# Moving columns of 512-wide products read from two halves in turn, PSUM read with a step of 2

## Chip, cores and metric

The kernel runs on one core of one Trainium2 chip. The metric is the device time of one execution in microseconds; lower is better. The time before is the median of three runs.

## What is computed

A trunk of two layers over 512 tokens with 1024 features, batch 1. Layer A mixes with a recurrent state per head (12 heads of 64) in parallel with a cross-attention into 256 memory tokens (4 heads); layer B mixes with attention in chunks of 64 tokens over the own chunk and 8 earlier ones, again beside a memory attention. Each layer then adds a gated channel mixer with a convolution over three tokens. Cut to what matters here:

```python
p = rms_norm(x, ln1[layer]) @ w_in                    # mixer columns | memory-query columns
mix = rwkv7_time_mix(h, p[..., :768 * 3], ...)        # layer A
mix = chunk_attention(q, k_pad, v_pad, bias)          # layer B
mo = memory_attention(q_mem, mem_n, w_mem_kv[layer])
x = x + concatenate([mix, mo]) @ w_out[layer]
gate, val = split(rms_norm(x, ln2[layer]) @ ffn_in[layer])
x = x + (gelu(conv3(gate)) * val) @ ffn_out[layer]
...
return rms_norm(x, ln_f)
```

All arithmetic is fp32. Large products are made of three single-pass products: each fp32 operand is split into a high part that the single pass takes exactly and a low rest, and high by high, high by low and low by high are summed in PSUM.

## The kernel before

Activations lie with features on the 128 partitions and the 512 tokens along the free axis: a tile `[128, 8, 512]` holds 1024 features. A weight tile holds 128 output features by 1024 inputs, in a high part `whi` (cast on ACT) and a low part `wlo` (subtracted on DVE, or fetched again by a DMA that adds).

`dense` makes one tile of 128 output features: for each of 8 feature blocks the weights are the stationary operand and 512 token columns are the moving one, first high weights by high and low activations (lines 241 and 242), then low weights by high activations (line 245): 24 products into one PSUM bank. It serves the projections of both mixers, the LoRA pairs, the output projections and the last tile of each channel mixer. Two banks (`psd`) take turns, so that a reader empties one while the other fills. Readers are DVE instructions for the most part: `proj` multiplies by the norm factor `rho` (line 1160), `out_proj` adds to the residual (line 407), `q_split` and `k_proj` scale queries and keys (1727 and 1742), `lora_pair`, `prepare` and `head_wide` do the like.

Stages, in order: mixer A (0 to 354 us; six head pairs, whose preparation, front and back are woven by a planner with costs written by hand), its output projection, the 21 tiles of the channel mixer's input products by a seven-product scheme with 256 columns each (`Seven`, line 434; with a last, plain tile in `ending`), and `out_by_seven`, the output products. In these, the activations are the stationary operand, 128 tokens at a time, and the weights `hi` and `lo` are the moving one, 512 output features wide (lines 698 and 703 in `rows`). Layer B repeats this with attention in place of the recurrence: `rows` in `attention` makes scores for 128 queries by 128 to 512 keys (lines 1788 and 1789), a DVE instruction adds the bias and finds the row's extreme in the same pass (line 1793), ACT exponentiates, DVE normalises, TensorE transposes, and the values are multiplied (line 1817). `mem_attention` does the same for the memory tokens; its value products (line 370) are plain fp32, not split, with 512 token columns.

The order of work on TensorE is that of the program text, with the planner's weaving of generators in the mixers. Loads of weights are issued by SyncE's queue; those that add are issued by GpSimd's.

Of the kernel before, what the change touches and what calls it, by code (L numbers as in the profile page):

```python
# [18 lines left out]
P = 128  # L19
S = 512  # L20
# [39 lines left out]
def _constants():  # L60
    f = np.float32
    c = np.zeros((P, NCST), f)

    def put(name, a):
        o, n = COFF[name]
        c[:, o:o + n] = a

    i = np.arange(P)
    same = (i[:, None] // 64) == (i[None, :] // 64)
    put("ident", np.eye(P, dtype=f))  # L70
    put("ones_d", np.full((P, 2), 1.0 / 1024, f))
# [12 lines left out]
    return c  # L84


# [35 lines left out]
def trunk_kernel(ctx, tc, A, out):  # L122
# [96 lines left out]

    def mm3(ps, wh, wl, ah, al, start, stop):  # L220
        PE.matmul(ps, wh, ah, start=start, stop=False)
        PE.matmul(ps, wh, al, start=False, stop=False)
        PE.matmul(ps, wl, ah, start=False, stop=stop)
# [6 lines left out]
    def behind_dense():  # L230
        return tc.issue_after(dense_at[0].ins)

    def dense(ps, units, act, order=None, start=True, stop=True):

        ks = [(w, j, k) for w, kk in units for j, k in enumerate(kk)]
        if order is not None:
            ks = [next(q for q in ks if q[2] == k) for k in order]

        for n, ((wh, wl), j, k) in enumerate(ks):
            ah, al = act(k)  # L240
            PE.matmul(ps, wh[:, j * P:(j + 1) * P], ah, start=start and n == 0, stop=False)  # L241
# [89 lines left out]
    def mem_attention(l, score, cost, dst, pr_tile, pt_tile):  # L331
# [66 lines left out]
    def out_proj(l, act, taken, xT, order, pre=(), done=()):  # L398
        for m in range(KD):
# [17 lines left out]
    def ffn(l, hp, U, T, new_x, xT, after=None, tokens=None):  # L417
# [29 lines left out]
        class Seven:  # L447
# [86 lines left out]
            def end5(self):  # L534
                keep(V.tensor_tensor(hid32[self.j], self.v[:], self.c[:], op=ALU.mult))

# [78 lines left out]
        def ending():  # L615
# [29 lines left out]
            g, c = tmp(), tmp()  # L645
            keep(V.tensor_tensor(g[:], pg[:], rho[:], op=ALU.mult))
            run(dense(pv[:], [(wv[:2], KO)], pair_of(Uh, Ul)))
            tile21 = Seven(j)
            tile21.g, tile21.c, tile21.v = g, c, pv
            tile21.end2()  # L650
# [41 lines left out]
        def rows(pss, act, k0, ch, first, last):  # L692
            hi, lo, n = ch
            for t, ps in pss:
                ts = slice(t * P, t * P + P)
                for i in range(n):
                    for a in act:
                        PE.matmul(ps[:], a[:, k0 + i, ts], hi[:, i * S:i * S + S],  # L698
                                  start=bool(first) and (first is True or t in first) and a is act[0] and i == 0, stop=False)
            for t, ps in pss:  # L700
                ts = slice(t * P, t * P + P)
                for i in range(n):
                    PE.matmul(ps[:], act[0][:, k0 + i, ts], lo[:, i * S:i * S + S], start=False, stop=bool(last) and t in last and i == n - 1)  # L703

# [310 lines left out]
    def lora_pair(idx, w, wm):  # L1015
# [5 lines left out]
        b_ = tmp()  # L1021
        V.tensor_tensor(b_[:], pb[:], rho[:], op=ALU.mult)
        z = tmp()
        V.tensor_tensor(z[:], pa[:], rho[:], op=ALU.mult)
        V.tensor_tensor(z[:], z[:], b_[:], op=ALU.subtract)
# [73 lines left out]
    def head_wide(src, fix, bank, tied=False):  # L1099
# [9 lines left out]
        fix(a[:], ps[:])  # L1109
        V.tensor_scalar(y[:].bitcast(I32), a[:].bitcast(I32), -0.5, 1597463007.0, op0=ALU.mult, op1=ALU.add)  # L1110
# [15 lines left out]
    def prepare(i, T):  # L1126
# [12 lines left out]
        pa = ps_s()  # L1139
        PE.matmul(pz[:], wah[:, 0], zw[:], start=True, stop=False)  # L1140
        PE.matmul(pa[:], wah[:, 1], zs[:], start=True, stop=False)
        PE.matmul(pz[:], wal[:, 0], zw[:], start=False, stop=True)
        PE.matmul(pa[:], wal[:, 1], zs[:], start=False, stop=True)
# [6 lines left out]
        SC.activation(th[:], pa[:], AF.Tanh, scale=0.5, bias=aw0h[:, i:i + 1])  # L1150

        def proj(j, nm, nxt):
# [107 lines left out]
        def bonus():  # L1260
# [7 lines left out]
            pb = ps_s()  # L1268
            PE.matmul(pb[:], blk1[:], rkh[:], start=True, stop=False)
            PE.matmul(pb[:], blk1[:], rkl[:], start=False, stop=True)  # L1270
            T["pb"] = pb
# [232 lines left out]
    def dst_mix(i, yc, pg):  # L1504
        V.tensor_tensor(yc[:], yc[:], pg[:], op=ALU.mult)
        if i < 4:
# [4 lines left out]
    def q_mem(src, act, qm):  # L1511
        for f in range(2):
            w = load_w(src(f))
            ps = ps_d()
            yield from dense(ps[:], [(w, K8)], act)
            V.scalar_tensor_tensor(qm[f], ps[:], 0.125, rho[:], op0=ALU.mult, op1=ALU.mult)

    def dst_mem(f, pso):
        SC.copy(r1h[:, 6 + f], pso[:])
        V.tensor_tensor(r1l[:, 6 + f], pso[:], r1h[:, 6 + f], op=ALU.subtract)  # L1520

# [164 lines left out]
    with ExitStack() as bctx:  # L1686
# [9 lines left out]

        def put_aside(m, src):
            t_ = tmp()
            SC.copy(t_[:], src)
            nc.sync.dma_start(mixb[m], t_[:])  # L1700
# [24 lines left out]
        def q_split(ps, T):  # L1725
            q = tmp()
            V.scalar_tensor_tensor(q[:], ps[:], 0.125, rho[:], op0=ALU.mult, op1=ALU.mult)

# [6 lines left out]
        def k_proj(i, T, ps=None):  # L1735
# [5 lines left out]
            k_ = tmp()  # L1741
            V.tensor_tensor(k_[:], ps[:], rho[:], op=ALU.mult)
            ks = ap_.tile([P, 2, S], F32R, name="ks", tag="ks")
# [29 lines left out]
        def attention(i, T):  # L1773
# [98 lines left out]
        def dst_memb(f, pso):  # L1872
            put_aside(6 + f, pso[:])
            done.add(f"m{f}")
# [85 lines left out]


def layout(i):
    g = {k: np.asarray(v) for k, v in i.items()}
# [34 lines left out]
    for l in range(2):  # L1998
# [33 lines left out]
```

## Time and profile before

| | |
|---|---|
| timed runs | 1291.62, 1292.89, 1293.07 us |
| median | 1292.89 us |
| span of the profiled execution, first to last instruction | 1292.6 us |
| granted TensorE clock, mean over the span | 0.997 |
| DMA, mean | 149 GB/s (192.14 MB) |
| HBM read | 174.20 MB |

The span leaves out what lies before the first and after the last instruction of the program; the profiled execution's span and the median of the timed runs differ by 0.3 us. In the rows of a profile "psf<-whi,th" names the tile written, then the tiles read; "128x512" is partitions by elements. A start time is counted from the start of the span. PE is TensorE, PEld its weight load, DVE VectorE, ACT ScalarE, POOL GpSimd, SP SyncE.

### The profile page before, as it was taken

Reading aid. Unit: us, or ns where it says so; the run is one execution under the profiler, and the core shown is the slowest. Engines: PE = TensorE matmul, PEld = TensorE weight load, DVE = VectorE, ACT = ScalarE, POOL = GpSimd, SP = SyncE. Lnnn points to the kernel's source line nnn. Section 1 sums busy time; section 2 is a strip of 40 time slices with the busy share of each in tenths; the row PEclk is TensorE's granted clock in tenths of the full one; section 3 lists DMA queues with packets and bytes.
Section 4 is the critical chain, followed back from the end, with each engine's and each line's share of the span. In section 5 each row is a group of like instructions: output and inputs, shape, how many; then the busy total and the mean of one; then the engine's idle time right before and its main releaser. Section 6 shows DMA issues by size and latency. Waiting matters only on the chain.

```text
span 1292.6 us, 26432 instructions
## 1 busy us (share of the span) xinstructions
PE 1260.9 (98%) x10420; PEld 1083.1 (84%) x10420; DVE 1031.7 (80%) x1956; ACT 846.4 (65%) x1398; POOL 152.7 (12%) x182
## 2 busy tenths in 40 slices
PE   9999999999999999999999999999999999999997
PEld 7887777777789999998888878787789999998886
DVE  7867677765688999998876876658889999998684
ACT  6566767856476777776554676757757777765662
POOL 1000000000001222320220000000002222211200
PEclk9999999999999999999999999999999999999999
DMA  5364444453055988996984322234429989978951
GB/s 204 110 174 106 100 96 89 92 109 96 30 166 126 212 198 198 206 208 172 274 185 122 118 87 82 76 104 123 130 61 212 197 193 211 208 161 262 233 149 66
DMA packets 95581, 192.14 MB, mean 149 GB/s; under 512 B 22112, under 2 KB 30432, under 8 KB 95456
## 3 DMA queue, kind: packets, MB, share of 16 engines
q1 hardware_dynamic: 68592, 129.14, 31.9%
q0 software_dynamic: 26864, 61.31, 27.3%
q8 instruction: 82, 1.34, 0.4%
q14 instruction: 43, 0.35, 0.1%
HBM read 174.20 MB, written 6.29 MB: 140 GB/s over the span
## 4 chain that ended last, share of the span: by engine, by line
PE 62%; DVE 15%; ACT 8%; DMA 8%; issue 6%; SPq 0%; POOL 0%; ACTq 0%; DVEq 0%; POOLq 0%
PE psf L434 8%; PE psf L698 7%; PE psd L245 6%; PE psd L241 5%; PE psd L242 5%; DMA wlv<-in_ffn_in_dram 4%; PE psf L436 4%; PE psf L703 4%; PE psd L698 3%; ACT whi L499 2%; DMA wraw<-in_ffn_in_dram 2%; PE psd L703 2%; DVE raw L486 1%; PE pss L1817 1%; DVE wlo L504 1%
## 5 line engine op out<-in xcount | busy, mean ns | idle before, releaser
L499 ACT CAST whi<-raw 128x1024 fp32r<-128x1024 f32 (+1 forms) x168 | 153.3, 942 | 62.3 <-PE psf L434 29.5
L434 PE MATMUL psf<-th,whi 128*128 128x256 f32 x672 | 161.4, 278 | 2.5 <-ACT tmp L553 1.9
L434 PE MATMUL psf<-tl,whi 128*128 128x256 f32 x672 | 161.1, 276 | 0.0
L195 ACT CAST whi<-wraw 128x1024 fp32r<-128x1024 f32 x84 | 87.6, 1048 | 78.3 <-PE psd L242 37.4
L434 PEld LDWEIGHTS psf<-th,whi 128*128 128x128 f32 x672 | 125.8, 188 | 3.9 <-ACT tmp L553 2.9
L434 PEld LDWEIGHTS psf<-tl,whi 128*128 128x128 f32 x672 | 126.0, 188 | 0.0
L504 DVE TENSOR_TENSOR wlo<-raw,whi 128x1024 fp32r<-128x1024 f32 (+1 forms) x108 | 109.3, 1012 | 9.1 <-ACT whi L499 8.9
L241 PE MATMUL psd<-r1h,whi 128*128 128x512 f32 x264 | 107.4, 408 | 0.0
L242 PE MATMUL psd<-r1l,whi 128*128 128x512 f32 x264 | 105.0, 398 | 0.0
L203 DVE TENSOR_TENSOR wlo<-wraw,whi 128x1024 fp32r<-128x1024 f32 x65 | 79.2, 1219 | 22.3 <-ACT whi L195 20.4
L688 ACT CAST whi<-raw 128x1024 fp32r<-128x1024 f32 (+1 forms) x52 | 49.6, 954 | 59.9 <-PE psf L698 33.1
L689 DVE TENSOR_TENSOR wlo<-raw,whi 128x1024 fp32r<-128x1024 f32 (+1 forms) x52 | 56.5, 1097 | 38.9 <-ACT whi L688 31.5
L436 PE MATMUL psf<-th,wlo 128*128 128x256 f32 x504 | 78.0, 276 | 0.0
L245 PE MATMUL psd<-r1h,wlo 128*128 128x512 f32 x264 | 74.3, 403 | 0.6 <-DMA wlo<-in_ffn_in_dram 0.4
L471 POOL DMA_DIRECT2D wlv<-in_ffn_in_dram x40 | 60.7, 1516 | 59.5 <-DVE tmp L572 59.1
L436 PEld LDWEIGHTS psf<-th,wlo 128*128 128x128 f32 x504 | 66.8, 188 | 0.0
L434 PE MATMUL psf<-r2h,whi 128*128 128x256 f32 x252 | 60.9, 278 | 0.7 <-ACT whi L499 0.7
L434 PE MATMUL psf<-r1h,whi 128*128 128x256 f32 x252 | 60.7, 277 | 0.7 <-ACT whi L499 0.7
L434 PE MATMUL psf<-r2l,whi 128*128 128x256 f32 x252 | 60.7, 277 | 0.0
L434 PE MATMUL psf<-r1l,whi 128*128 128x256 f32 x252 | 60.6, 277 | 0.0
L241 PEld LDWEIGHTS psd<-r1h,whi 128*128 128x128 f32 x264 | 49.6, 188 | 12.0 <-issue 2.1
L525 ACT ACTIVATE tmp<-tmp,vec 128x512 f32<-128x512 f32 x44 | 36.0, 817 | 33.3 <-DVE tmp L512 33.3
(611 smaller groups left out, 3576.8 us busy)
## 6 DMA issues: line engine op xcount, KB each, us to landing
raw<-in_ffn_in_dram SPq DMA_DIRECT2D x42, 512.0 KB, 5.2
raw<-in_ffn_in_dram SPq DMA_DIRECT2D x84, 256.0 KB, 5.5
wlv<-in_ffn_in_dram POOLq DMA_DIRECT2D x40, 512.0 KB, 8.6
raw<-in_ffn_out_dram SPq DMA_DIRECT2D x30, 512.0 KB, 6.2
raw<-in_ffn_out_dram POOLq DMA_DIRECT2D x24, 512.0 KB, 8.4
wraw<-in_wA_dram SPq DMA_DIRECT2D x20, 512.0 KB, 4.1
wraw<-in_w_out_dram SPq DMA_DIRECT2D x16, 512.0 KB, 4.1
wraw<-in_ffn_outp_dram SPq DMA_DIRECT2D x16, 512.0 KB, 4.5
```

Of the source, the lines that this page charges most:

```text
L195: high = lambda: pin(SC.copy(hi[:, :n], raw))
L203: pin(V.tensor_tensor(lo[:, :n], raw, hi[:, :n], op=ALU.subtract))
L241: PE.matmul(ps, wh[:, j * P:(j + 1) * P], ah, start=start and n == 0, stop=False)
L242: dense_at[0] = PE.matmul(ps, wh[:, j * P:(j + 1) * P], al, start=False, stop=False)
L245: dense_at[0] = PE.matmul(ps, wl[:, j * P:(j + 1) * P], act(k)[0], start=False, stop=stop and n == len(ks) - 1)
L434: PE.matmul(ps, wh[:, o + k * P:o + k * P + P], x[k][n], start=k == n == 0, stop=False)
L436: PE.matmul(ps, wl[:, ol + k * P:ol + k * P + P], x[k][0], start=False, stop=k == 3)
L471: GP.dma_start(self.low[:].rearrange("p (a s) -> p a s", a=2), self.second, accum_op=ALU.add)
L499: keep(SC.copy(hi[:, :n], self.pair(what) if n > S else self.raw[:, what]))
L504: keep(V.tensor_tensor(lo[:, :n], self.pair(what) if n > S else self.raw[:, what], hi[:, :n], op=ALU.subtract))
L698: PE.matmul(ps[:], a[:, k0 + i, ts], hi[:, i * S:i * S + S], start=bool(first) and (first is True or t in first) and a is act[0] and i == ...
L703: PE.matmul(ps[:], act[0][:, k0 + i, ts], lo[:, i * S:i * S + S], start=False, stop=bool(last) and t in last and i == n - 1)
```

## The change

Three views are added. `woven` reads a tile of n columns as column 0, column n/2, column 1, column n/2 + 1 and so on. A product whose moving operand is woven puts its results in that order, so `plain_order` reads PSUM as even columns and then odd ones, a step of 2 with two runs, and `halved` gives the other operand and the output the same shape, two contiguous halves.

The moving operand becomes woven in `dense` (where it has 512 columns), `mm3`, the value products of `mem_attention`, `rows` of the output products, `head_wide`, the four products at the head of `prepare`, the bonus, and the scores of the two wider query tiles (384 and 512 keys). For the output products no reader changes: the weights `ffn_out7` and `ffn_outp` are laid out beforehand so that the woven read gives plain order. Every other reader of such a bank takes `plain_order`. Products of 256 columns, the transposes and the values of the chunked attention stay as they are.

```diff
+def woven(t):
+    return t.rearrange("p (a b) -> p b a", a=2)
+
+def halved(t):
+    return t.rearrange("p (a b) -> p a b", a=2)
+
+def plain_order(ps):
+    return ps.rearrange("p (b a) -> p a b", a=2)
...
     def mm3(ps, wh, wl, ah, al, start, stop):
+        ah, al = woven(ah), woven(al)
...
+    def moving(hl):
+        return [woven(t) if t.shape[-1] == S else t for t in hl]
...
-            ah, al = act(k)
+            ah, al = moving(act(k))
...
-            dense_at[0] = PE.matmul(ps, wl[:, j * P:(j + 1) * P], act(k)[0], start=False,
+            dense_at[0] = PE.matmul(ps, wl[:, j * P:(j + 1) * P], moving(act(k))[0], start=False,
...
-                    PE.matmul(pso[hs, :], vm[l][:, kt, (f * 2 + hh) * 64:(f * 2 + hh + 1) * 64], pts[f, hh, kt],
+                    PE.matmul(pso[hs, :], vm[l][:, kt, (f * 2 + hh) * 64:(f * 2 + hh + 1) * 64], woven(pts[f, hh, kt]),
...
-            V.tensor_tensor(xT[:, m], xT[:, m], ps[:], op=ALU.add)
+            V.tensor_tensor(halved(xT[:, m]), halved(xT[:, m]), plain_order(ps[:]), op=ALU.add)
...
-                        PE.matmul(ps[:], a[:, k0 + i, ts], hi[:, i * S:i * S + S],
+                        PE.matmul(ps[:], a[:, k0 + i, ts], woven(hi[:, i * S:i * S + S]),
...
-                    PE.matmul(ps[:], act[0][:, k0 + i, ts], lo[:, i * S:i * S + S], start=False, stop=bool(last) and t in last and i == n - 1)
+                    PE.matmul(ps[:], act[0][:, k0 + i, ts], woven(lo[:, i * S:i * S + S]), start=False, stop=bool(last) and t in last and i == n - 1)
...
-            PE.matmul(ps[:], blk1[:], hi[:], start=True, stop=False)
-            PE.matmul(ps[:], blk1[:], lo[:], start=False, stop=True)
+            PE.matmul(ps[:], blk1[:], woven(hi[:]), start=True, stop=False)
+            PE.matmul(ps[:], blk1[:], woven(lo[:]), start=False, stop=True)
...
-        SC.activation(sig[:], pz[:], AF.Tanh, scale=0.5, bias=aw0h[:, 6 + i:7 + i])
+        SC.activation(halved(sig[:]), plain_order(pz[:]), AF.Tanh, scale=0.5, bias=aw0h[:, 6 + i:7 + i])
...
-            V.tensor_tensor(p_[:], ps[:], rho[:], op=ALU.mult)
+            V.tensor_tensor(halved(p_[:]), plain_order(ps[:]), halved(rho[:]), op=ALU.mult)
...
-        V.tensor_tensor(bon[:], T["pb"][:], T["v"][:], op=ALU.mult)
+        V.tensor_tensor(halved(bon[:]), plain_order(T["pb"][:]), halved(T["v"][:]), op=ALU.mult)
...
+                mix, flat_, sorted_ = (woven, halved, plain_order) if qt > 1 else (lambda t: t,) * 3
...
-                PE.matmul(ps[:, :n], qs[:, hh, qc], ks[:, hh, :n], start=True, stop=False)
-                PE.matmul(ps[:, :n], qs[:, hh, qc], kl[:, hh, :n], start=False, stop=True)
+                PE.matmul(ps[:, :n], qs[:, hh, qc], mix(ks[:, hh, :n]), start=True, stop=False)
+                PE.matmul(ps[:, :n], qs[:, hh, qc], mix(kl[:, hh, :n]), start=False, stop=True)
...
-                V.tensor_tensor_reduce(sb[:, :n], ps[:, :n], big[hh][:, S - n:S], -1.0, 3e38,
+                V.tensor_tensor_reduce(flat_(sb[:, :n]), sorted_(ps[:, :n]), flat_(big[hh][:, S - n:S]), -1.0, 3e38,
...
+def _woven(w):
+
+    return np.ascontiguousarray(w.reshape(*w.shape[:-1], -1, S // 2, 2).swapaxes(-1, -2)).reshape(w.shape)
...
-    A["ffn_out7"] = np.stack(seven)
-    A["ffn_outp"] = np.stack(plain)
+    A["ffn_out7"] = _woven(np.stack(seven))
+    A["ffn_outp"] = _woven(np.stack(plain))
```

The lines left out give the remaining readers of a woven bank (the last tile of the channel mixer, the LoRA pair, the memory query, the output of the memory attention, queries and keys of layer B, the gate of mixer A) the same three views, and nothing else.

More of the change, by code (lines that the diff above doesn't have):

```diff
@@ L534, in end5 @@
             def end5(self):
-                keep(V.tensor_tensor(hid32[self.j], self.v[:], self.c[:], op=ALU.mult))
+                v = self.v if self.j == NFF - 1 else halved(self.v[:])
+                keep(V.tensor_tensor(halved(hid32[self.j]), v, halved(self.c[:]), op=ALU.mult))
             def frame(self, prev2, prev, nxt, norm=None, ending=None):
@@ L645, in ending @@
             g, c = tmp(), tmp()
-            keep(V.tensor_tensor(g[:], pg[:], rho[:], op=ALU.mult))
+            keep(V.tensor_tensor(halved(g[:]), plain_order(pg[:]), halved(rho[:]), op=ALU.mult))
             run(dense(pv[:], [(wv[:2], KO)], pair_of(Uh, Ul)))
             tile21 = Seven(j)
-            tile21.g, tile21.c, tile21.v = g, c, pv
+            tile21.g, tile21.c, tile21.v = g, c, plain_order(pv[:])
             tile21.end2()
@@ L1021, in lora_pair @@
         b_ = tmp()
-        V.tensor_tensor(b_[:], pb[:], rho[:], op=ALU.mult)
+        V.tensor_tensor(halved(b_[:]), plain_order(pb[:]), halved(rho[:]), op=ALU.mult)
         z = tmp()
-        V.tensor_tensor(z[:], pa[:], rho[:], op=ALU.mult)
+        V.tensor_tensor(halved(z[:]), plain_order(pa[:]), halved(rho[:]), op=ALU.mult)
         V.tensor_tensor(z[:], z[:], b_[:], op=ALU.subtract)
@@ L1105, in head_wide @@
         with behind_dense() if tied else ExitStack():
-            PE.matmul(ps[:], blk1[:], hi[:], start=True, stop=False)
-            PE.matmul(ps[:], blk1[:], lo[:], start=False, stop=True)
+            PE.matmul(ps[:], blk1[:], woven(hi[:]), start=True, stop=False)
+            PE.matmul(ps[:], blk1[:], woven(lo[:]), start=False, stop=True)
         a, y, sh = tmp(), tmp(), tmp()
-        fix(a[:], ps[:])
+        fix(halved(a[:]), plain_order(ps[:]))
         V.tensor_scalar(y[:].bitcast(I32), a[:].bitcast(I32), -0.5, 1597463007.0, op0=ALU.mult, op1=ALU.add)
@@ L1139, in prepare @@
         pa = ps_s()
[L1140 to L1143, printed above, removed]
+        PE.matmul(pz[:], wah[:, 0], woven(zw[:]), start=True, stop=False)
+        PE.matmul(pa[:], wah[:, 1], woven(zs[:]), start=True, stop=False)
+        PE.matmul(pz[:], wal[:, 0], woven(zw[:]), start=False, stop=True)
+        PE.matmul(pa[:], wal[:, 1], woven(zs[:]), start=False, stop=True)
         yield 860
         sig = tmp()
-        SC.activation(sig[:], pz[:], AF.Tanh, scale=0.5, bias=aw0h[:, 6 + i:7 + i])
+        SC.activation(halved(sig[:]), plain_order(pz[:]), AF.Tanh, scale=0.5, bias=aw0h[:, 6 + i:7 + i])
         V.tensor_scalar(sig[:], sig[:], 0.5, 0.5, op0=ALU.mult, op1=ALU.add)
         th = kt_("a")
-        SC.activation(th[:], pa[:], AF.Tanh, scale=0.5, bias=aw0h[:, i:i + 1])
+        SC.activation(halved(th[:]), plain_order(pa[:]), AF.Tanh, scale=0.5, bias=aw0h[:, i:i + 1])
         def proj(j, nm, nxt):
@@ L1268, in bonus @@
             pb = ps_s()
-            PE.matmul(pb[:], blk1[:], rkh[:], start=True, stop=False)
-            PE.matmul(pb[:], blk1[:], rkl[:], start=False, stop=True)
+            PE.matmul(pb[:], blk1[:], woven(rkh[:]), start=True, stop=False)
+            PE.matmul(pb[:], blk1[:], woven(rkl[:]), start=False, stop=True)
             T["pb"] = pb
@@ L1504, in dst_mix @@
     def dst_mix(i, yc, pg):
-        V.tensor_tensor(yc[:], yc[:], pg[:], op=ALU.mult)
+        V.tensor_tensor(halved(yc[:]), halved(yc[:]), plain_order(pg[:]), op=ALU.mult)
         if i < 4:
@@ L1515, in q_mem @@
             yield from dense(ps[:], [(w, K8)], act)
-            V.scalar_tensor_tensor(qm[f], ps[:], 0.125, rho[:], op0=ALU.mult, op1=ALU.mult)
+            V.scalar_tensor_tensor(halved(qm[f]), plain_order(ps[:]), 0.125, halved(rho[:]), op0=ALU.mult, op1=ALU.mult)
     def dst_mem(f, pso):
-        SC.copy(r1h[:, 6 + f], pso[:])
-        V.tensor_tensor(r1l[:, 6 + f], pso[:], r1h[:, 6 + f], op=ALU.subtract)
+        SC.copy(halved(r1h[:, 6 + f]), plain_order(pso[:]))
+        V.tensor_tensor(halved(r1l[:, 6 + f]), plain_order(pso[:]), halved(r1h[:, 6 + f]), op=ALU.subtract)
     def flush_mix():
@@ L1695, in trunk_kernel, with put_aside @@
         nc.sync.dma_start(vm1, kv1[1])
-        def put_aside(m, src):
+        def put_aside(m, src, view=lambda t: t):
             t_ = tmp()
-            SC.copy(t_[:], src)
+            SC.copy(view(t_[:]), src)
             nc.sync.dma_start(mixb[m], t_[:])
@@ L1726, in q_split @@
             q = tmp()
-            V.scalar_tensor_tensor(q[:], ps[:], 0.125, rho[:], op0=ALU.mult, op1=ALU.mult)
+            V.scalar_tensor_tensor(halved(q[:]), plain_order(ps[:]), 0.125, halved(rho[:]), op0=ALU.mult, op1=ALU.mult)
             qs = ap_.tile([P, 2, S], F32R, name="qs", tag="qs", bufs=3)
@@ L1741, in k_proj @@
             k_ = tmp()
-            V.tensor_tensor(k_[:], ps[:], rho[:], op=ALU.mult)
+            V.tensor_tensor(halved(k_[:]), plain_order(ps[:]), halved(rho[:]), op=ALU.mult)
             ks = ap_.tile([P, 2, S], F32R, name="ks", tag="ks")
@@ L1872, in dst_memb @@
         def dst_memb(f, pso):
-            put_aside(6 + f, pso[:])
+            put_aside(6 + f, plain_order(pso[:]), halved)
             done.add(f"m{f}")
```

## The prediction

> **What bounds the kernel now.** I read the page first (busy times, then the chain that ended last), then the busy time by stretches, cut where the stages change.
>
> ```profile
> PE 1260.9 (98%) x10420; PEld 1083.1 (84%) x10420; DVE 1031.7 (80%) x1956; ACT 846.4 (65%) x1398; POOL 152.7 (12%) x182
> ...
> PE 62%; DVE 15%; ACT 8%; DMA 8%; issue 6%; SPq 0%; POOL 0%; ACTq 0%; DVEq 0%; POOLq 0%
> ```
> ```profile
> 0.00:354.00 354.00, 343.18 (x4360) 265.94 (x4361) 252.98 (x682) 230.17 (x453) 18.33 (x36) 1.00 0.44 109
> 354.00:394.00 40.00, 39.89 (x191) 33.34 (x189) 31.86 (x50) 26.04 (x37) 1.75 (x2) 1.00 0.46 146
> 394.00:604.00 210.00, 206.42 (x1766) 203.37 (x1767) 198.62 (x302) 151.69 (x201) 50.61 (x49) 1.00 0.85 191
> 604.00:712.00 108.00, 107.83 (x483) 88.91 (x483) 80.73 (x85) 58.90 (x73) 13.88 (x16) 1.00 0.75 197
> 712.00:918.00 206.00, 201.99 (x1145) 159.90 (x1144) 145.85 (x370) 138.34 (x318) 2.01 (x12) 1.00 0.31 97
> 918.00:953.00 35.00, 35.00 (x171) 29.58 (x171) 30.62 (x50) 24.34 (x36) 1.74 (x2) 1.00 0.33 96
> 953.00:1165.00 212.00, 206.49 (x1771) 203.39 (x1770) 198.31 (x301) 152.93 (x201) 50.56 (x49) 1.00 0.85 189
> 1165.00:1276.00 111.00, 110.79 (x504) 91.34 (x503) 83.67 (x90) 59.02 (x77) 13.87 (x16) 1.00 0.70 187
> ```
> The columns are stretch, length, then busy time with instruction count of PE, weight load, DVE, ACT, POOL, and granted clock, DMA share, GB/s. The stages are mixer A, its output projection, the input products of the first channel mixer, its output products, then the same four for layer B. TensorE is never off for long in any of them, at full clock; in the two output-product stages (604 and 1165) DVE is busy three quarters and ACT half of the time. So a cheaper product is worth nearly its whole saving wherever its PE time is not under a wait.
>
> What does one product cost? The chain of waits in order of time shows the output products back to back, and the timeline gives the other widths:
>
> ```profile
> 610.36 3.63 PE psf L698 x16
> 613.99 1.81 PE psf L703 x8
> 615.80 3.63 PE psf L698 x16
> 619.42 1.81 PE psf L703 x8
> 621.24 3.63 PE psf L698 x16
> ```
> ```profile
> 548.17 0.28 PE L434 MATMUL psf<-r2h,whi 128*128 128x256 f32 x1
> ...
> 548.96 0.28 PE L434 MATMUL psf<-r2l,whi 128*128 128x256 f32 x1
> ```
> ```profile
> 310.97 1.46 PE L1590 MATMUL pss<-kmT,kn 64*128 64x256 f32 x6
> ```
> ```profile
> L1590 PE MATMUL pss<-kmT,kn x16: 376/376/480, 310.6 to 317.9; 64*128 64x256 f32 x16
> ```
> From 610.36 to 621.24 lie 48 products of 512 columns: 10.88/48 = **226.7 ns** each. Those of 256 columns start (548.96-548.17)/7 = 113 ns apart, the same 0.443 ns per column. The scores of line 1590 are plain fp32: the kernel makes 8 of them from `kn` with 256 columns and the row has 16 records, so a record is taken as two passes over its columns. Six records fill 1.46 us, the last takes 0.376 (median), so starts lie (1.46-0.376)/5 = **216 ns** apart for 512 column passes. TensorE can therefore take 512 columns in 216 ns when each column read serves two passes; the single pass pays 10.7 ns more, about one part in twenty. That is all this change can be after in the product itself.
>
> **The change part by part.** (1) *The moving operand in another order.* Number of single-pass products of 512 columns, from the stretch view over the whole span for each line (lines 241, 242, 245, 698, 703, in this order; PE busy and count):
>
> ```profile
> 0.00:1293.00 1293.00, 195.94 (x496) 1.00 0.60 149
> 0.00:1293.00 1293.00, 192.03 (x496) 1.00 0.60 149
> 0.00:1293.00 1293.00, 132.27 (x496) 1.00 0.60 149
> 0.00:1293.00 1293.00, 161.90 (x648) 1.00 0.60 149
> 0.00:1293.00 1293.00, 86.52 (x324) 1.00 0.60 149
> ```
> Of each 496, 32 are memory keys with 256 columns, which stay as they are: 3x464 + 648 + 324 = 2364. By the code come 18 (gates, mm3), 8 (head_wide), 24 (decay and rate), 12 (bonus), 24 (scores of the last query tile): **2450**, and 24 scores of 384 columns. No row of this trace has a moving operand that jumps at every column, so the price has two ends. Best end: the reader's surcharge goes and a single pass costs what half of a two-pass read shows, 216: 2450 x 10.7 = 26.2 us, and 24 x 8 = 0.2. Worst end: a jump per column halves the read rate, 2 x 216 = 432 ns, 2450 x 205 = 503 us more. I take 216. The reason is the two rows above: the product is short of its natural pace by a small, even share at every place and width, which looks like a stream that trips at regular steps along one run of addresses; two runs in turn step half as often each. This is an inference, and nothing here shows the two-run read itself.
>
> The nearest row for word-by-word jumps speaks against it, on another engine:
>
> ```profile
> L1233 DVE TENSOR_TENSOR Xu<-Lr,cst 128x120 f32<-128x120 f32 x6 | 2.1, 356 | 2.9 <-DMA Lr<-d 2.9
> ...
> L1446 DVE TENSOR_TENSOR MQ<-pss,cst 128x256 f32<-128x256 f32 x10 | 4.2, 419 | 7.5 <-PE pss L1445 7.5
> ...
> L1303 DVE TENSOR_TENSOR ML<-pss,cst 128x512 f32<-128x512 f32 x24 | 16.2, 684 | 0.4 <-PE pss L1300 0.4
> ```
> Contiguous tensor_tensor costs (684-419)/256 = 1.035 ns per element, so 120 elements would take 278 ns; line 1233 reads one input with a step of 16 words and takes 356: 0.65 ns more per element. [...]
>
> (2) *Readers of PSUM with step 2.* By the code 98 DVE instructions (18 projections at line 1160, 16 residual adds at 407, 24 wide scores at 1793, the rest q, k, LoRA, bonus, gates) and 18 of ACT. Without a row for a step in PSUM: nothing, or the 0.65 ns of line 1233, which is 333 ns per 512 elements, 98 x 0.333 = 33 us of DVE. Almost all of it is beside TensorE: the projection's bank has a second one to go on with, and in mixer A DVE has 100 us free. Cover is thinnest in the second output projection: DVE 30.62 of 35 us; with 8 x 0.333 it is 33.3, while TensorE falls to 35 - 192 x 0.0107 = 32.9. There DVE would be late next, by 0.4 us. Plus the softmax chain, some ten instructions at its ends: on the path I put **1.5 us** (0 to 5).
>
> (3) *Weights woven beforehand* for the output products: the same bytes and DMAs, no reader with a step, nothing.
>
> (4) *Memory values*: plain fp32, two passes to a record, already at the pace that I take as the floor. Nothing.
>
> (5) *What comes late.* In the mixers lie 998 of the products (638 + 360), worth 10.7 us; TensorE idles 11 of 354 and 4 of 206 us there, waiting for chains of small steps that do not shorten; I give back a sixth, 1.8 us. In the stages of input products only the 96 of the last tile change, and half of these end before a wait for the value weights,
>
> ```profile
> 595.70 6.77 DMA wraw<-in_ffn_in_dram
> ```
> which swallows 48 x 10.7 = 0.5 us. No DMA, queue or added wait moves otherwise.
>
> **Sum.** 26.2 + 0.2 - 0.5 - 1.8 - 1.5 = 22.6 us. The profiled execution spans 1292.6 us, the timed runs have a median of 1292.89, so it stands for them within 0.3: 1292.9 - 22.6 = **1270 us**, 1.7% faster.
>
> Own range of this case:
>
> ```profile
> L241 PE MATMUL psd<-r1h,whi 128*128 128x512 f32 x264 | 107.4, 408 | 0.0
> ...
> L698 PE MATMUL psf<-whi,th 128*128 128x512 f32 x96 | 37.4, 389 | 0.0
> ```
> The 1392 products of `dense` last 19 ns longer than those back to back, for stalls among them. With nothing given back (26.4) and a sixth of these 19 ns gone too (4.4), 1262. Up to 1286 if two streams meet the weight load badly, which this trace shows to cost something:
>
> ```profile
> 750.50 0.28 PE L1767 MATMUL pss<-whi,r1h 128*128 128x256 f32 x1
> ...
> 755.69 0.28 PE L1769 MATMUL pss<-wlo,r1h 128*128 128x256 f32 x1
> ```
> These 44 steps of 118 ns read other tiles than the 113 ns ones, same shape: 5 ns by place alone. 2450 x (10.7 - 5) = 14, less 0.5, 1.8 and 5 is 6.7.
>
> **Rivals.** *First, the jump itself is paid* (slower). Place: every woven product; price: half rate, 432 ns, 1293 + 503 = **1796 us**. It decides from 0.443 ns per column on, the present cost. [...] *Second, the surcharge does not come from the read order*, so the change doesn't do what it says: products stay at 226.7 and only readers cost, 0 to 5 us: **1293 to 1298**. For it: the surcharge is the same for weights that lie at different offsets, so it may be the pace of a single pass as such. *Third, gain eaten by the weight load*, above: 1286, still faster.
>
> **How the numbers follow.** Forecast with the third: 0.68. Second: 0.12, of which 0.08 within 0.2% (about what a measurement of this kernel tells from no change) and 0.04 above. First: 0.20, all slower. So faster 0.68, same 0.08, slower 0.24. The range takes in the forecast's own range and the second rival and leaves out the first: 1260 to 1298.
>
> **What would show it.** Starts of lines 698 and 703 at 216 ns (right), 227 (second rival), well above 300 (first). Lines 407 and 1160 at 683 ns if the step in PSUM is free, near 1020 if not; DVE of the second output projection then over 95% busy. The stages 604 and 1165 each shorter by about 5 us, the stages 394 and 953 unchanged. Wrong would be: products faster but mixers as long as before, or ones that change their pace by the tile they read.

## The result and the profile after

The changed kernel takes 1275.62 us, the median of four runs (1273.37 to 1277.75), beside 1292.82 us for the kernel before on the same chip: a ratio of 0.9872, 95% interval 0.9856 to 0.9887. That is 17.2 us less, where 22.6 us were forecast. The time lies in the range, the sign is the forecast one, and a quarter of the expected gain is missing.

The page of the kernel after, busy times and the chain that ended last:

```profile
PE 1233.5 (97%) x10420; PEld 1084.3 (85%) x10420; DVE 1031.0 (81%) x1956; ACT 846.8 (66%) x1398; POOL 152.9 (12%) x182
...
PE 45%; DVE 25%; ACT 12%; issue 10%; DMA 7%; SPq 0%; ACTq 0%; POOL 0%; DVEq 0%; POOLq 0%
```

Counts of instructions are those of before. TensorE's busy time fell by 27.4 us (from 1260.9), but the span only by 16.6 (1292.6 to 1276.0), so TensorE now idles 42.5 us instead of 31.7. The chain says the same in another way: TensorE holds 45% of it where it held 62%, and DVE and ACT have taken its place. The busy times of DVE, ACT and POOL moved by 0.7 us at most.

The chain in order of time, at the head of the first output products:

```profile
607.05 3.45 PE psf L715 x16
610.50 1.73 PE psf L720 x8
612.23 3.45 PE psf L715 x16
615.68 1.73 PE psf L720 x8
```

Lines 715 and 720 are lines 698 and 703 of before. 48 products take 2 x (3.45 + 1.73) = 10.36 us, 215.8 ns each, where they took 226.7. The readers of PSUM, from the costliest groups (line 1177 was 1160, line 423 was 407; each is shown after, then before):

```profile
L1177 DVE TENSOR_TENSOR tmp<-psd,rho 128x512 f32<-128x512 f32 x18 | 12.3, 684 | 0.5 <-PE psd L261 0.4
L423 DVE TENSOR_TENSOR xT<-xT,psd 128x512 f32<-128x512 f32 x12 | 8.1, 683 | 8.7 <-DMA xT<-in_xT_dram 4.6 <-PE psd L261 4.1
```
```profile
L1160 DVE TENSOR_TENSOR tmp<-psd,rho 128x512 f32<-128x512 f32 x18 | 12.3, 683 | 0.6 <-PE psd L245 0.5
L407 DVE TENSOR_TENSOR xT<-xT,psd 128x512 f32<-128x512 f32 x12 | 8.1, 683 | 11.5 <-PE psd L245 7.2 <-DMA xT<-in_xT_dram 4.3
```

The step of 2 in PSUM costs DVE nothing: 684 and 683 ns against 683 and 683. So the product is cheaper and its reader is not dearer, and what is missing must be looked for by stage. The stretches of the kernel after, cut within an instruction or two of those of before (columns are stretch, length, then busy time with count of PE, weight load, DVE, ACT, POOL, then clock, DMA share, GB/s):

```profile
0.00:351.30 351.30, 335.76 (x4360) 266.05 (x4361) 252.93 (x682) 229.64 (x453) 18.35 (x36) 1.00 0.44 110
351.30:390.20 38.90, 38.16 (x190) 33.51 (x189) 31.58 (x50) 25.57 (x37) 1.75 (x2) 1.00 0.49 151
390.20:600.50 210.30, 205.79 (x1767) 203.06 (x1767) 198.83 (x303) 153.25 (x201) 50.62 (x49) 1.00 0.86 191
600.50:703.50 103.00, 102.48 (x483) 89.47 (x482) 80.05 (x84) 58.66 (x72) 13.88 (x16) 1.00 0.78 207
703.50:907.80 204.30, 197.71 (x1147) 159.67 (x1146) 146.16 (x370) 138.60 (x319) 2.16 (x12) 1.00 0.31 97
907.80:941.20 33.40, 33.40 (x171) 29.70 (x170) 30.73 (x50) 24.19 (x36) 1.75 (x2) 1.00 0.34 102
941.20:1154.00 212.80, 206.06 (x1771) 203.63 (x1770) 198.18 (x301) 153.07 (x201) 50.56 (x49) 1.00 0.85 189
1154.00:1259.90 105.90, 105.39 (x505) 91.91 (x504) 83.47 (x90) 58.84 (x77) 13.88 (x16) 1.00 0.73 197
```

| stage | before, us | after, us | gain | forecast | after, again, us |
|---|---|---|---|---|---|
| two mixers | 560.0 | 555.6 | 4.4 | 998 products x 10.7 ns - 1.8 = 8.9 | 554.7 |
| two output projections | 75.0 | 72.3 | 2.7 | 384 x 10.7 ns = 4.1 | 73.1 |
| two stages of input products | 422.0 | 423.1 | -1.1 | 96 x 10.7 ns - 0.5 = 0.5 | 419.2 |
| two stages of output products | 219.0 | 208.9 | 10.1 | 972 x 10.7 ns = 10.4 | 208.6 |
| the rest | 16.6 | 16.1 | 0.5 | | 15.8 |
| sum | 1292.6 | 1276.0 | 16.6 | 23.9, + 0.2 of scores - 1.5 of readers = 22.6 | 1271.4 |

The last column is the same kernel, profiled once more (the first run of the next section). It shows how far a single execution can be trusted: the mixers and the output products repeat within 1 us, the input products differ by 3.9 us.

Where products stand in one unbroken row, the whole gain arrived (10.1 of 10.4). In the mixers it did not: the first needs 7.4 us less TensorE time (343.18 to 335.76) and is 2.7 us shorter, the second 4.3 us less (201.99 to 197.71) and 1.7 us shorter. The theory to test: chains of small steps on DVE and ACT set part of the mixers' pace, so that a microsecond of TensorE time is worth only part of one there. The rival: the new read order costs something in the mixers (a slower product, the memory values), and the time would come back without it.

### The profile page after: what moved, and what is told of

Same layout as the page of the kernel before. It is cut to its first block, busy times and chain, and to the rows that moved or that the text cites. A ratio compares the mean times of both kernels' runs of the same rounds, so it can differ in the third digit from the quotient of the medians.

```text
span 1276.0 us, 26437 instructions
## 1 busy us (share of the span) xinstructions
PE 1233.5 (97%) x10420; PEld 1084.3 (85%) x10420; DVE 1031.0 (81%) x1956; ACT 846.8 (66%) x1398; POOL 152.9 (12%) x182
## 3 DMA queue, kind: packets, MB, share of 16 engines
q0 software_dynamic: 26864, 61.31, 27.4%
## 4 chain that ended last, share of the span: by engine, by line
PE 45%; DVE 25%; ACT 12%; issue 10%; DMA 7%; SPq 0%; ACTq 0%; POOL 0%; DVEq 0%; POOLq 0%
PE psf L715 7%; PE psd L261 4%; PE psf L720 3%; PE psd L257 3%; PE psd L258 3%; PE psd L715 3%; PE psf L450 3%; ACT whi L515 3%; DVE raw L502 2%; DMA wlv<-in_ffn_in_dram 2%; DVE wlo L215 2%; DVE wlo L520 2%; DVE raw L511 2%; DVE tmp L525 2%; PE psd L720 1%
## 5 line engine op out<-in xcount | busy, mean ns | idle before, releaser
L257 PE MATMUL psd<-r1h,whi 128*128 128x512 f32 x264 | 104.0, 395 | 0.0
L258 PE MATMUL psd<-r1l,whi 128*128 128x512 f32 x264 | 101.6, 386 | 0.0
L261 PE MATMUL psd<-r1h,wlo 128*128 128x512 f32 x264 | 70.6, 390 | 2.6 <-DMA wlo<-in_ffn_in_dram 1.3
L261 PEld LDWEIGHTS psd<-r1h,wlo 128*128 128x128 f32 x264 | 47.7, 189 | 10.3 <-DVE wlo L215 1.8
```

The source lines that it names most:

```text
L261: dense_at[0] = PE.matmul(ps, wl[:, j * P:(j + 1) * P], moving(act(k))[0], start=False, stop=stop and n == len(ks) - 1)
```

## The experiments

**The change by itself, again, and without the woven memory values.** The first kernel is the changed one, unaltered; the second takes one edit back (and its readers with it):

```diff
-  PE.matmul(pso[hs, :], vm[l][:, kt, ...], woven(pts[f, hh, kt]),
+  PE.matmul(pso[hs, :], vm[l][:, kt, ...], pts[f, hh, kt],
```

> The changed kernel itself, on the chip of the other runs of this group, as their yardstick. 17 us below the kernel before (1275.6 against 1292.8 in the first comparison). Its product with 512 single-pass columns starts every 216 ns.

> The changed kernel with the memory values (plain fp32, two passes to a record) read in plain order again. Theory: a two-pass product reads each column once for two passes, has no surcharge to lose, and the woven read costs it time; pairs of these products go back from about 531 ns to 429 ns, 16 pairs, so 1.5 to 2 us faster than the changed kernel. Rival: the other engines' chain around the values decides there, and the whole time stays within 0.5 us of the changed kernel.

The changed kernel gave 1273.48 us, 0.9862 (0.9842 to 0.9882) of before's 1291.98: 18.5 us. With plain values 1272.96, 0.9853 (0.9837 to 0.9870). The memory values themselves, from the timelines: first the changed kernel, then the one with plain values.

```profile
802.36 2.38 PE L386 MATMUL pss<-ptT,vm 128*64 128x512 f32 x8
```
```profile
800.59 1.94 PE L386 MATMUL pss<-ptT,vm 128*64 128x512 f32 x8
```

Eight records are four products, by the kernel's 16 of them and the view's 32 records. Woven they take 0.44 us more, 0.11 us a product, 1.8 us of TensorE time for the 16 by this row. So the weave makes the plain fp32 product slower, which the prediction had at nothing. The whole time moves by only 0.5 us, but its intervals are about 2 us wide to either side and can't tell 0.5 from 1.8. The stretch around the values can, since the order of TensorE's instructions is the same in both kernels. In mixer A, from the first value product to the product that follows the last one, again first the changed kernel, then the one with plain values:

```profile
330.60 1.83 PE L386 MATMUL pss<-KB,vm 128*64 128x512 f32 x5
...
345.53 0.66 PE L1108 MATMUL pss<-cst,tmp 128*128 128x128 f32 x4
```
```profile
329.14 1.50 PE L386 MATMUL pss<-KB,vm 128*64 128x512 f32 x5
...
342.96 0.66 PE L1108 MATMUL pss<-cst,tmp 128*128 128x128 f32 x4
```

That is 14.93 us against 13.82, and 14.92 in the repeated profile: 1.10 us. In layer B the same stretch runs from 802.36 to 817.81 and from 800.59 to 815.39, 15.45 us against 14.80: 0.65 us. Together 1.75 us, so the mixers hide nothing of the 1.8. That the theory's 1.5 to 2 us hold is read from these stretches; the whole times leave them open, and its reason, one read of a column for two passes, is not shown. The loss explains about a third of the missing 5 us.

**Only the output products, and everything but them.** The first is the kernel before with `rows` woven and the weights laid out to suit; the second is the changed kernel with these taken back.

```diff
-  PE.matmul(ps[:], a[:, k0 + i, ts], hi[:, i * S:i * S + S],
+  PE.matmul(ps[:], a[:, k0 + i, ts], woven(hi[:, i * S:i * S + S]),
...
-  A["ffn_out7"] = np.stack(seven)
+  A["ffn_out7"] = _woven(np.stack(seven))
```

> The kernel before with only the 972 output products of the channel mixers woven and their weights laid out beforehand; no reader of PSUM changes. Theory: there TensorE sets the pace alone, so 972 x 10.9 ns = 10.6 us come off, 1282.2. Rival: the splitting on ACT and DVE sets the pace in part, and 5 us or less come off, 1288 or more.

> The changed kernel with the output products and their weights in plain order again: 1478 products of the mixers, projections and last tiles woven. At 10.9 ns each they would give 16.1 us. Theory: more than half is lost to waits in the mixers, at the start and before the first input products, so 5 to 8 us come off, 1285 to 1288. Rival: they give all of it and the output products give little, so 14 us or more come off.

Measured: 1281.70 us, 0.9917 (0.9903 to 0.9932), and 1284.09 us, 0.9938 (0.9921 to 0.9955). So the output products bring 10.3 us of the 972 x 10.9 ns = 10.6 that their count asks for, and all the rest 7.9 us of 1478 x 10.9 = 16.1. The two add up to 18.2, the whole change's 18.5: they do not help or hinder each other, and the shortfall lies whole in the second part.

**What a us of TensorE time is worth in a mixer.** First by taking work out: in the eighteen projections of mixer A the third pass (low weights by high activations) is left out.

```diff
-  yield from dense(ps[:], [(w, K8)], hact)
+  yield from dense(ps[:], [(w, K8)], hact, low=False)
```

> The changed kernel without the third pass (low weights by high activations) in the 18 projections of mixer A; the low weights are still made. This leaves out 144 products, 144 x 215.8 ns = 31.1 us of TensorE time, and less exact results. It asks what an us of TensorE time is worth in mixer A. Theory: chains of small steps set much of the pace there, so about 40% comes off the whole as it did for the change itself, 12 us (8 to 16): near 1261. Rival: TensorE sets the pace there and the change's gain was lost in other stages, so 27 us or more come off: below 1247.

It took 1286.93 us, 0.9957 (0.9934 to 0.9979), slower than the changed kernel that has 31 us more to do. Both theories fall, since each wanted time to come off. The stretches of its mixer A against those of the changed kernel, first the kernel without the pass:

```profile
100.00:150.00 50.00, 38.33 (x616) 28.51 (x614) 30.07 (x77) 32.58 (x60) 5.16 (x6) 0.90 0.59 128
...
300.00:350.00 50.00, 48.56 (x714) 37.93 (x706) 24.64 (x76) 24.77 (x70) 0.00 (x0) 0.76 0.14 39
```
```profile
100.00:150.00 50.00, 46.78 (x786) 35.86 (x786) 35.31 (x83) 32.22 (x65) 3.29 (x4) 1.00 0.47 99
...
300.00:350.00 50.00, 49.81 (x676) 36.53 (x676) 32.37 (x97) 27.69 (x77) 0.00 (x0) 1.00 0.10 34
```

With less to do TensorE idled more (38.33 of 50 us busy in the first of these stretches) and its granted clock fell to 0.90 there and once, later, to 0.76. Summed over the seven stretches of 50 us from 0 to 350, (1 - clock) x 50 us is an estimated 28.5 us of clock not granted, and 2.0 in the changed kernel: nearly what the pass left out is worth. Moreover the order of work on TensorE, DVE and ACT came out different from the changed kernel's, although the planner's costs, written by hand, stayed as they were; what moved it is not shown. So two things changed that were to stay, and the run does not separate them. It does show a lower granted clock beside more idle time in the first pair of rows (0.90 against 1.00, 38.33 against 46.78 us busy). That the idle time brought it on is not shown; beside 0.76 TensorE was busy for 48.56 of 50 us.

Then by putting work in, with every instruction in its place: mixer A's projections read four runs in turn instead of two.

```diff
-  yield from dense(ps[:], [(w, K8)], hact)
+  yield from dense(ps[:], [(w, K8)], hact, a=4)
...
-  V.tensor_tensor(halved(p_[:]), plain_order(ps[:]), halved(rho[:]), op=ALU.mult)
+  V.tensor_tensor(four(p_[:]), ps[:].rearrange("p (b a) -> p a b", a=4), four(rho[:]), op=ALU.mult)
```

> The changed kernel, and in mixer A alone the 432 products of 512 columns of its eighteen projections read their columns from four runs in turn instead of two, their readers stepping to suit. In the run with ten orders such a product took 283 ns where two runs take 216, so TensorE gets 432 x 67 ns = 29 us more work in mixer A, and no instruction of any engine changes its place. It prices a us of TensorE time in the mixer. If chains on the other engines set a large part of the pace of the mixer, as half of the lost gain there says: 12 to 22 us of the 29 are added, 1286 to 1296 us in all. If TensorE sets the pace in the mixers too, and the gain was lost for another reason: 27 us or more, 1300 us and above.

It took 1291.22 us, 0.9998 (0.9987 to 1.0009): 15.6 us over the changed kernel's first median and 17.7 over its second. Its mixer A:

```profile
0.00:366.70 366.70, 358.18 (x4360) 265.85 (x4361) 253.91 (x682) 229.99 (x453) 18.34 (x36) 1.00 0.42 105
```

The mixer is 15.4 us longer (366.7 against 351.3) for 22.4 us more busy time and, by count and price, 29 us more work: 15 to 16 of 29 us arrive, as the theory had it. In the other direction the change took 638 x 10.9 ns = 7.0 us out of this mixer by count, and 2.7 us came off (350.4 us long in the repeated profile, so 3.6 there). The memory values put 1.1 us on in this mixer; without them the other products brought 3.8 and 4.7 of 7.0 us, 54 and 67%. Half to two thirds is the round figure for both directions, though it isn't one constant. What gave way are waits: TensorE's idle time in this mixer is 10.8 us before (354.00 less 343.18), 15.5 in the changed kernel and 8.5 with four runs. Of the 13.6 us that do not arrive with four runs, 7.0 fill idle time; the rest lies within the busy time, where these rows do not show it. TensorE's waits on two of the chains (us in all, times, longest): before, after, and with four runs, in this order.

```profile
PE pss L1375 <- ACT Y L1364: 1.2, 5, 0.3
...
PE pss L1091 <- DVE tmp L1088: 0.4, 2, 0.2
```
```profile
PE pss L1392 <- ACT Y L1381: 1.8, 5, 0.5
...
PE pss L1108 <- DVE tmp L1105: 1.0, 3, 0.3
```
```profile
PE pss L1108 <- DVE tmp L1105: 0.3, 1, 0.3
```

Line 1375 is line 1392 after, line 1091 is 1108. TensorE's wait for ACT's copy of `Y` grows from 1.2 to 1.8 us when the products beside it get shorter and is gone from the list when they get longer; the wait for DVE's `tmp` goes 0.4, 1.0, 0.3. Many waits of this kind, none of them large, make up the 4.7 us by which the idle time grew.

**Which orders are cheap.** The kernel before, its output products read in ten orders by turns: plain, then in 2, 4, 8, 16, 32, 64, 128 and 256 runs in turn, then pairs of columns from two halves. The outputs keep these orders.

```diff
+  far = lambda m, a: m.rearrange("p (a b) -> p b a", a=a)
...
+  elif o == 2:
+      PE.matmul(ps, w, far(m, 4), start=start, stop=stop)
```

> The kernel before, with the output products read in ten orders in turn, one per block of weights: plain; 2, 4, 8, 16, 32, 64, 128 or 256 runs in turn (steps of 1024, 512, 256, 128, 64, 32, 16 and 8 bytes); and pairs of neighbours from two halves. Output features come out in another order, so the result is not the reference's. Theory A, a stream that trips at regular steps along one run: orders with far steps (1024 down to 64 bytes) at 216 ns, steps of 8 and 16 bytes at 227 like the plain one, pairs at 216. [...]

The chain in order of time, one line of the kernel for each order:

```profile
609.50 5.45 PE psf L698 x24
614.95 5.18 PE psf L700 x24
620.13 6.79 PE psf L702 x24
626.92 5.87 PE psd L704 x12
632.79 5.22 PE psd L706 x12
...
651.34 5.42 PE pss L714 x12
656.75 4.00 PE pss L716 x12
```

| order | ns a product |
|---|---|
| plain (698) | 5.45/24 = 227 |
| two runs (700) | 216 |
| four runs (702) | 283 |
| eight runs (704) | 489 |
| sixteen runs (706) | 435 |
| 32, 64, 128 runs (708, 710, 712) | 433, 432, 462 |
| 256 runs, a step of two (714) | 452 |
| pairs from two halves (716) | 333 |

The whole kernel took 1411.02 us this way, in a single run. Only two runs are cheaper than plain. Theory A falls: it has two runs right (216 ns), but it wanted 216 for four to 32 runs and for the pairs as well, which take 283 to 489 and 333, and 227 for 128 and 256 runs, which take 462 and 452. From four runs on the product is slower than plain, but not the slower the more runs there are: eight runs (489) cost more than sixteen (435).

**Do the two runs have to lie far apart?** The kernel before, output products in two runs at distances of 256, 128, 64, 32, 16 and 8 columns (lines 706 to 716), at 512, 257 and 272 (718 to 722), and a plain run that starts at an odd word (724). Outputs keep these orders here too.

```diff
+  def near(m, d):
+      return m.rearrange("p (c a b) -> p c b a", a=2, b=d)
...
+  elif o == 5:
+      PE.matmul(ps, w, near(m, 8), start=start, stop=stop)
...
+      PE.matmul(ps, w, full[:, i * 256 + 1:i * 256 + 513], start=start, stop=stop)
```

> The kernel before, with the output products read in ten orders in turn, one per block of two weight tiles: two runs in turn that lie 256, 128, 64, 32, 16 or 8 columns apart (1024 down to 32 bytes), 512 columns apart (2048 bytes, one half from each of two tiles), 257 columns and 272 columns apart (1028 and 1088 bytes), and one run that begins at an odd word. Output features come out in another order or from other columns, so the result is not the reference's. [...] Theory E, the two runs must lie in different parts of the memory that repeat with some distance: 216 for 1024 bytes and slower, towards the 433 ns of many runs, for the shorter distances. Theory F, the order matters only through the pairing of words of 8 bytes: 1028 bytes apart differs from 1024.

The chain in order of time:

```profile
613.52 5.18 PE psf L706 x24
...
634.24 2.59 PE psd L716 x12
...
638.23 2.59 PE pss L718 x12
640.82 2.60 PE pss L720 x12
...
647.38 5.68 PE psf L724 x24
```

256 columns, 8 columns (32 bytes), 512 columns, an odd distance of 257: 216 or 217 ns, each of them; the whole kernel took 1288.17 us, in a single run. E and F fall: where the two runs lie makes no difference. Nor is it enough to read from two places in turn: the pairs of the run before do that too and take 333. The plain run from an odd word takes 5.68/24 = 237 ns, where plain products took 227 in the run before. That the odd word costs this is not shown: plain products differ by place, and the plain blocks from even words between these orders take 1.39/6 = 232 in the same chain. Why two runs are cheaper than one and four dearer, no run here shows.

**The 256-column products too.** The changed kernel with plain memory values, and the seven-product scheme's products woven as well, their readers stepping by 2:

```diff
-  PE.matmul(ps, wh[:, o + k * P:o + k * P + P], x[k][n], start=k == n == 0, stop=False)
+  PE.matmul(ps, wh[:, o + k * P:o + k * P + P], woven(x[k][n]), start=k == n == 0, stop=False)
```

> The changed kernel with memory values in plain order and the products of 256 columns (the seven-product scheme) woven as well, their readers with a step of 2. Theory: the narrow products pay the same sixteenth (113.3 ns); the next bound is the weight load at about 108 ns, so 5 ns come off each of 4032, 20 us of TensorE; DVE is busy 95% of those stages, so only 6 to 12 us come off the whole beyond the kernel with plain values. Rival: 113 ns is the weight load's own pace, and nothing comes off.

It took 1271.53 us, 0.9835 (0.9814 to 0.9856): the lowest median of all, yet its interval overlaps those of the changed kernel and of the one with plain values. The chain of the input products, first the version with plain values, then this one:

```profile
515.94 0.91 PE psf L450 x8
516.85 0.45 PE psf L452 x4
```
```profile
515.41 0.89 PE psf L450 x8
516.31 0.45 PE psf L452 x4
```

Eight products take 0.89 instead of 0.91 us: 111 ns against 114, where half of 216 would be 108. So 2 ns come off and not 5, and the whole time doesn't tell: the rival is nearly right. The theory's 108 ns for a weight load and its sixteenth were estimates of the author's that no row shows; 10.7 of 226.7 ns is one part in 21. That the columns do not set this floor can be read from the kernel before, where eight products move 2 columns each, with a weight load of 128 columns for each:

```profile
338.56 0.95 PE L1082 MATMUL pss<-cst,tmp 128*128 128x2 f32 x8
339.44 0.48 PE L1590 MATMUL pss<-kmT,kh 64*128 64x256 f32 x1
```

From the first of them to the next product lie 0.88 us, 110 ns a product. So a product with its own load of 128 columns takes about 110 ns even when only 2 columns move, and the woven 256-column product has come down to that (111), which points to the load, or something that goes with it, and not to the columns. In this stage the chain also waits for weights (one step of it reads `501.52 9.44 DMA wlv<-in_ffn_in_dram` in the version with plain values), so little would come of it in any case.

## Why the prediction was right, and where it was off

**Step 1, the product at 216 ns: right.** 215.8 in the trace. The value came from the plain fp32 scores of line 1590, and it held for the woven single-pass products of 512 columns. That a record of line 1590 is two passes, and that each column is read once for both, was the author's reading of 16 records for 8 products; no run shows it. Nor is the reason given, a stream that trips at regular steps, shown: two runs take 216 or 217 ns at every distance, but "two runs in turn step half as often each" would have promised more from four, and four cost 283.

**Step 2, readers: mechanism bounded rightly, value too high.** 1.5 us was put on the path; the step costs 0 or 1 ns per DVE instruction, so the term is nothing. The row it was bounded by, line 1233, steps 16 words in SBUF and does not stand for a step of 2 in PSUM. By luck this error made up for 1.5 us of what was lost elsewhere.

**Step 3, the host-woven weights: right.** The output products by themselves brought 10.3 of 10.6 us.

**Step 4, memory values "already at the pace that I take as the floor. Nothing": wrong.** A woven plain fp32 product is 0.11 us slower, 1.8 us of TensorE time for 16 of them, and the stretches around them are 1.75 us longer: a term put at nothing that cost about as much as the whole of step 5 was to give back. The error was to take "two passes" and "two runs" for the same gain, since both show 216; together they cost 0.11 us a product.

**Step 5, what comes late: right in kind, mis-sized, and the term that failed.** A sixth, 1.8 of 10.7 us, was to be given back in the mixers. Their stretches gained 4.4 us (5.3 in the repeated profile), so 6.3 (5.4) were given back, 4.5 (3.6) more than put. Of these 1.75 are the memory values; the chains took the other 4.5 (3.6), two to two and a half times the 1.8. The sixth was read from TensorE's idle time in the mixers, 11 of 354 and 4 of 206 us. That is the wrong measure: idle time says how much the chains cost already, not how much more they will once the products that cover them shrink. The run with four runs in turn gives a better one: about half of a microsecond arrives.

**The input products: "no DMA, queue or added wait moves otherwise" was wrong.** The 96 woven products of the last tiles were to win 1.0 us and lose 0.5 to one wait; they won nothing. From the last 256-column product to the first output product the ends of both stages take 25.5 us before (597.41 to 610.20 and 1158.34 to 1171.07), 26.1 after and 25.8 in the repeated profile. The timeline of TensorE there, before and after, shows in brackets what each group waited for:

```profile
602.33 2.12 PE L245 MATMUL psd<-r2h,wlo 128*128 128x512 f32 x8 [0.54 <-DMA wlo<-in_ffn_in_dram]
608.25 2.11 PE L245 MATMUL psd<-r2h,wlo 128*128 128x512 f32 x8 [0.17 <-DVE wlo L203]
...
1163.16 2.12 PE L245 MATMUL psd<-r1h,wlo 128*128 128x512 f32 x8 [0.43 <-DMA wlo<-in_ffn_in_dram]
1169.11 2.12 PE L245 MATMUL psd<-r1h,wlo 128*128 128x512 f32 x8 [0.21 <-DVE wlo L203]
```
```profile
599.09 1.99 PE L261 MATMUL psd<-r2h,wlo 128*128 128x512 f32 x8 [0.81 <-DMA wlo<-in_ffn_in_dram]
605.05 1.99 PE L261 MATMUL psd<-r2h,wlo 128*128 128x512 f32 x8 [0.52 <-DVE wlo L215]
...
1152.25 1.99 PE L261 MATMUL psd<-r1h,wlo 128*128 128x512 f32 x8 [1.33 <-DMA wlo<-in_ffn_in_dram]
1158.20 1.99 PE L261 MATMUL psd<-r1h,wlo 128*128 128x512 f32 x8 [0.51 <-DVE wlo L215]
```

The high weights' products end sooner, and TensorE waits longer for the low weights: 3.2 us instead of 1.4, 1.8 more. That swallows more than the 1.0 us that these products saved. The same four waits are 2.9 us in the repeated profile, but 2.0 in the kernel with everything but the output products woven. The two for DVE are steady, 0.5 us each in these three kernels and 0.2 before; the two for a DMA differ between executions.

The 1.1 us that the two stages lose in the table is not the change's doing. From their first to their last 256-column product, which the change leaves as they are, they take 418.8 us before, 420.0 after, 416.8 in the repeated profile and 415.7 with only the output products woven. One of the waits that differ is that of the seven-product scheme for ACT's `tmp`: 1.9 us in all before, 4.6 after and 1.6 in the repeated profile.

The corrections to 22.6 by the table of stages: +1.5 for readers, -4.5 for the mixers, -1.6 for the input products, -1.4 for the output projections, -0.3 for the output products, -0.2 for the scores, +0.5 for the rest: 16.6, the span's difference. Of the 1.6 about one is the variation just named; in the repeated profile the same sum ends at 21.2, with +2.3 for the input products and -3.6 for the mixers. The 1.4 of the output projections are the least certain, as their cuts fall between instructions that do not match to better than one or two; the stretch of the second holds 171 instructions both times and is 1.6 us shorter.

**The rivals.** The first, a jump that is paid, has its direction from four runs on (283 to 489 ns, where 432 was its price), and its decisive point, 0.443 ns a column, was well chosen; at two runs the product is cheaper (216). That a jump per column halves the rate was the author's assumption, which no row of before shows: sixteen to 64 runs came to 432 to 435, two runs did not. For it to have 0.20 was fair on what the trace showed. The second, an unchanged pace, fell with the first row of line 715. The third, gain eaten by the weight load, fell for 512 columns; something of its kind holds the 256-column products at 111, as the products of 2 columns at 110 suggest.

## What to carry to other kernels

A TensorE product that reads its columns from two runs in turn can be cheaper than one that reads a single run (216 against 227 ns for 512 single-pass columns here), and the step of 2 that its readers then need in PSUM cost DVE nothing (684 and 683 ns against 683); four runs (283 ns), or two runs with plain fp32 products (2.38 against 1.94 us for four), lost. Price such a gain by stage. Here it came whole where products stand in one unbroken row (10.1 of 10.4 us), half to two thirds where they cover chains of small steps on other engines (54 and 67% in the first mixer), however little TensorE seems to idle there, and not at all where the next operand has its own time of arrival (1.8 us more of waits for 1.0 us saved). To price a microsecond of an engine in a stage, add work without moving an instruction; taking work out can change the order and the clock along with it, as it did here (0.76 in one stretch).

## What the runs showed of the hardware that was not expected

- Two runs in turn: 216 or 217 ns at every distance tried, from 32 bytes to 2 KB; plain 227, four runs 283, eight 489, pairs of columns from two halves 333.
- Plain fp32 products of 512 columns lose by two runs in turn: 2.38 instead of 1.94 us for four of them.
- Products of 2 columns, each with its own weight load of 128 columns, take 110 ns each (0.88 us for eight); those of 256 columns 114, woven 111.
- DVE's reads of PSUM with a step of 2 take as long as contiguous ones: 684 and 683 ns against 683.
- With 31 us of TensorE work left out of the first mixer, the granted clock fell to 0.76 in one stretch of 50 us, and the kernel became slower than the one that does the work (1286.93 us against 1275.62 and 1273.48). The order of work changed too, so the clock's share is open.
